# Summing a gate's modulation over partitions with one full-width TensorE product a stream, instead of quarter-width products and a trip through DRAM

## The chip, the cores and the metric

The kernel runs on one core of one Trainium2 chip. The metric is the device time of one execution in microseconds (us). The kernel before takes 1478.86 us, the median of 3 runs (1477.71 to 1479.12). TensorE is called PE here, VectorE DVE, ScalarE ACT, GpSimd POOL and SyncE SP, as in the profile. A wait of an instruction is given by the profile as idle time of its engine, with the instruction or transfer that ended it.

## The reference

The model is a two-layer trunk over 256 context tokens and 256 latent tokens of width 1024. Every layer has an attention part with three mixers (MLA, differential attention, sliding-window attention called SWA) and a SwiGLU part. Each part is modulated by six vectors that come from the condition:

```
def adaln(cond, w, b):
    return jnp.split(jax.nn.silu(cond) @ w + b, 6, axis=-1)

def modulate(h, shift, scale):
    return h * (1.0 + scale) + shift
# per layer: shift1, scale1, gate1, shift2, scale2, gate2
#   x = x + gate1 * rms_norm(mixers(...), attn_post_norm)
#   x = x + gate2 * rms_norm(swiglu(...), ffn_post_norm)
```

The change concerns the two gate vectors, number 2 and number 5 of the six. The kernel stores a gate already multiplied with its norm weight and with 32, the square root of 1024, so that the residual is one product more.

## The kernel before, in words

All matrix products of the blocks run on PE with the weights split into a high and a low part: three matmuls per product, recorded at lines L262, L263 and L264 and accumulated in PSUM (`psg`). Weight blocks are loaded by SP into `raw` buffers (L170), cast by ACT (L131, the high part) and subtracted by DVE (L132, the low part, both called `hl`). Only then can PE use them.

The modulation is computed on DVE beside this work, by the generator `ada_dve`. The weights of a vector's half (512 columns) come as four tiles `aw` of 128 partitions (L342 issues them on SP). Partition p and tile j hold rows of the weight matrix; DVE multiplies each with the activated condition of that partition and adds it into `acc` (L397 and L399), one 512-column accumulator for each stream (`ns` = 2: latent and context, or `ns` = 1 in the last layer's gates). What is left is the sum over the 128 partitions. `finish` does it: products with a 128 x 32 block of ones (L357) sum 256 columns each into 32 partitions of PSUM, and ACT copies the sums to SBUF (L359).

For shift and scale vectors the sums are then transposed on PE. For a gate the sum must stand on every partition. There `finish` writes one row per 256 columns to DRAM (L362), reads it back broadcast to 128 partitions into the tile `gw` (L371), and loads the bias and the norm weight in the same broadcast form into two buffers of the `work` pool (L375 and L376). All four transfers are issued by SP. Then DVE adds the bias (L379) and multiplies with 32 and the weight (L380).

The `work` pool has six buffers of 128 x 512 that all engines share in turn, for exponentials, normed products and the like. A buffer is handed on when its last reader has finished.

The order of the work is set by the order in which the program is written and by generators that yield costs in microseconds. `start_fill` starts one `ada_dve` run beside the main sequence, and `fillers` advances it by the cost of what PE has been given. There are four such runs. The first (layer 0, beside its mixers) makes vectors 4, 3 and gate 2 with two streams. The second (beside the SwiGLU of layer 0) makes gate 5 with two streams and vectors of layer 1. The third and fourth make gate 2 and gate 5 of layer 1 with one stream. So there are eight gate halves: four with two streams and four with one. A `finish` is itself a generator (`pend`): it is advanced by `next(pend, None)` between the `aw` tiles of the following half, at high priority, and after each step the run is charged 0.3, 0.3 and, for a gate, `1.0 * ns`.

Of the kernel before, what the change touches and what calls it, by code (L numbers as in the profile page):

```python
# [10 lines left out]
F32 = mybir.dt.float32  # L11
# [3 lines left out]
ALU = mybir.AluOpType  # L15
# [4 lines left out]
P = 128  # L20
D = 1024
# [66 lines left out]
def trunk(ctx: ExitStack, tc: tile.TileContext, x, cx, b_ada, attn_post,  # L88
          ffn_post, w_in, w_uq, w_ukv, diff_lambda, swa_sink,
          w_ba, w_bb, w_bc, w_o, w_gu, w_dn, const_a, const_b, ada_first, ada_rest, out, dram_in):  # L90
    nc = tc.nc
# [5 lines left out]
    dp = ctx.enter_context(tc.tile_pool(name="dp", bufs=1, space=DRAM))  # L97
# [4 lines left out]
    def bank(tag="g"):  # L102
        return pp.tile([P, 512], F32, tag=tag, bufs=BANKS[tag], name=f"ps{tag}")
# [7 lines left out]
    def work():  # L111
        return sp.tile([P, 512], F32, tag="w2", bufs=6, name="work")
# [4 lines left out]
    ident, sel_f = ca[:, 0:128], ca[:, 128:130]  # L117
# [4 lines left out]
    ones = cp.tile([P, P], F32, name="ones")  # L122
# [193 lines left out]
    mods = {}  # L316

    def mod_finish(l, kind, f0, m, pv):

        nf, ns = pv.shape[1:]  # L320
        o = l * 48 + kind * 8 + f0
        b = bt[:, o:o + nf].rearrange("p (f o) -> p f o", o=1).to_broadcast([P, nf, ns])
        mq = m[:, f0:f0 + nf, :ns]
        nc.vector.tensor_tensor(mq, pv, b, ALU.add)
        if kind in (1, 4):
            off = (VAP if kind == 1 else VFP) + 8 * l + f0
            w = vt[:, off:off + nf].rearrange("p (f o) -> p f o", o=1).to_broadcast([P, nf, ns])
            nc.vector.scalar_tensor_tensor(mq, mq, 1.0, w, ALU.add, ALU.mult)

    def mod_tile(kind):  # L330
        return cp.tile([P, KD, 2], F32, tag=f"mod{kind}", name=f"mod{kind}")

    def ada_dve(*jobs):


        H = D // 2
        todo = [(l, kind, ns, hf) for l, kind, ns in jobs for hf in range(2)]

        def raw(i, j):
            l, kind, _, hf = todo[i]  # L340
            w = sp.tile([P, 2, H], F32, tag="xt", bufs=2, name="aw")
            nc.sync.dma_start(w.rearrange("p k n -> p (k n)"), ada_rest[l, kind, hf, j])  # L342
            return w

        def finish(l, kind, ns, hf, acc):
            m = mods[l, kind]
            gate = kind in (2, 5)
            n = 64 * ns
            ps = bank("T")
            for g in range(2):  # L350
                for s in range(ns):
                    j = 32 * (2 * s + g if gate else ns * g + s)
                    if gate:
                        src = acc[:, s, g * 256:(g + 1) * 256]
                    else:
                        src = acc[:, s].rearrange("p (b g c) -> p b g c", b=2, g=2)[:, :, g]
                    nc.tensor.matmul(ps[j:j + 32, :256], lhsT=ones[:, :32], rhs=src, start=True, stop=True)  # L357
            sums = work()[:, :256]
            nc.scalar.copy(sums[:n], ps[:n, :256])  # L359
            if gate:  # L360
                row = dp.tile([2 * ns, 256], F32, name=f"row{l}_{kind}_{hf}")
                nc.sync.dma_start(row, sums[0:n:32])  # L362
            yield
            if not gate:
                ps = bank("T")
                for b in range(2):
                    nc.tensor.transpose(ps[:, b * n:(b + 1) * n], sums[:n, b * P:(b + 1) * P], ident[:n, :n])
                mod_finish(l, kind, 4 * hf, m, ps[:, :2 * n].rearrange("p (f s z) -> p f s z", s=ns, z=32)[:, :, :, 0])
                return
            mq = m[:, :ns, hf * H:(hf + 1) * H]  # L370
            nc.sync.dma_start(mq, row.rearrange("(s g) p -> s (g p)", s=ns).rearrange("(o s) n -> o s n", o=1).to_broadcast([P, ns, H]))  # L371
            bw = [work(), work()]
            w = attn_post if kind == 2 else ffn_post
            c0 = kind * D + hf * H
            nc.sync.dma_start(bw[0], b_ada[l:l + 1, c0:c0 + H].to_broadcast([P, H]))  # L375
            nc.sync.dma_start(bw[1], w[l:l + 1, hf * H:(hf + 1) * H].to_broadcast([P, H]))  # L376
            yield
            for s in range(ns):
                nc.vector.tensor_tensor(mq[:, s], mq[:, s], bw[0], ALU.add)  # L379
                nc.vector.scalar_tensor_tensor(mq[:, s], mq[:, s], 32.0, bw[1], ALU.mult, ALU.mult)  # L380

        nxt = raw(0, 0)
        pend = None
        for i, (l, kind, ns, hf) in enumerate(todo):
            if hf == 0:
                gate = kind in (2, 5)
                mods[l, kind] = bp.tile([P, 2, D], F32, tag="gw", bufs=1, name="gw") if gate else mod_tile(kind)
            acc = sp.tile([P, 2, H], F32, tag="acc", bufs=2, name="acc")
            for j in range(4):
                w = nxt  # L390
                if j < 3 or i + 1 < len(todo):
                    nxt = raw(i + j // 3, (j + 1) % 4)
                for k in range(2):
                    for s in range(ns):
                        sc = siluc[:, s, 2 * j + k:2 * j + k + 1]
                        if j == 0 and k == 0:
                            nc.vector.tensor_scalar(acc[:, s], w[:, k], sc, None, ALU.mult)  # L397
                        else:
                            nc.vector.scalar_tensor_tensor(acc[:, s], w[:, k], sc, acc[:, s], ALU.mult, ALU.add)  # L399
                    yield 0.76 * ns  # L400
                if j and pend is not None:
                    with tc.high_priority():
                        next(pend, None)
                    yield (0.3, 0.3, 1.0 * ns if kind in (2, 5) else 0.0)[j - 1]
            pend = finish(l, kind, ns, hf, acc)
        for _ in range(3):
            yield 2.0
            with tc.high_priority():
                next(pend, None)
# [3 lines left out]
    for t in range(4):  # L413
        src = cx if t < 2 else x
# [1023 lines left out]
    for l in range(DEPTH):  # L1438
# [20 lines left out]
        if l == 0:  # L1459
            later = [(30.0, lambda: start_fill(ada_dve((0, 4, 2), (0, 3, 2), (0, 2, 2)), FR[0]))]  # L1460
        else:
            later = ()
            start_fill(ada_dve((1, 2, 1)), FR[2])
# [12 lines left out]
        for i, t in enumerate(qts):  # L1476
            ch = L[l]["ch", qts[i - 1]] if i else None
            a, b = PRM["WO"][2 * l:2 * l + 2]
            drive(1, at=[(a, lambda: next(ch, None)), (b, lambda: next(ch, None))] if i else ())
        ch = L[l]["ch", qts[-1]]  # L1480
        if not last:
            drive(1, at=[(a, lambda: next(ch, None)) for a in PRM["WO"][4:]])
            start_fill(ada_dve((0, 5, 2), (1, 1, 2), (1, 0, 2), (1, 4, 1), (1, 3, 1)), FR[1])
        else:
            warm(WN[0])
            next(ch, None)
            next(ch, None)
            warm(WN[1])
            start_fill(ada_dve((1, 5, 1)), FR[3])
# [47 lines left out]
```

## Time and profile before

| what | value |
|---|---|
| median of 3 runs | 1478.86 us |
| the profiled execution, its own time | 1479.64 us |
| its span, first to last instruction | 1477.9 us |
| granted PE clock, mean over the span | 0.995 of full speed |
| PE busy | 1437.3 us, 97% |
| DVE busy | 969.3 us, 66% |
| ACT busy | 684.3 us, 46% |
| POOL busy | 175.8 us, 12% |

The shares are averages over stages that differ. A time in the rows below counts from the start of the span. Matmuls overlap in their pipeline, so what a matmul costs is read from the distance between the starts of the matmuls around it, not from its own duration. A float32 matmul call leaves two records, a split product one record in each of three lines.

### The profile page before, as it was taken

How to read it: one execution, taken by the hardware profiler on the slowest of the kernel's cores; microseconds unless marked ns; L12 is line 12 of the kernel's file. 1: busy time of each engine (PE TensorE's matmuls, PEld its weight loads, DVE VectorE, ACT ScalarE, POOL GpSimd, SP SyncE). 2: the span in 40 equal slices, each digit the busy share in tenths (PEclk: the TensorE clock that was granted, in tenths of full speed). 3: DMA queues.
4: the chain of work that ended last, by engine and by line, in shares of the span. 5: the costliest groups of instructions: out<-in, count | busy, mean ns of one | idle time of the engine just before them, and what ended most of it. 6: DMA issues, size and time to landing. Idle time of an engine off the chain costs nothing. (4 is left out here: it accounts for less than half of the span.)

```text
span 1477.9 us, 21889 instructions
## 1 busy us (share of the span) xinstructions
PE 1437.3 (97%) x8434; PEld 1213.7 (82%) x8434; DVE 969.3 (66%) x1646; ACT 684.3 (46%) x1265; POOL 175.8 (12%) x245
## 2 busy tenths in 40 slices
PE   8989999999999999999999999999999899999998
PEld 7867878777777889887778888878798899899986
DVE  4676777878785655879773224779577776666644
ACT  5576554444552355223222123765455655544443
POOL 1262001220000010000000000364013100100000
PEclk9999999999999999999999999999999999999999
DMA  9321322233223542666572324333242426566664
GB/s 351 123 80 43 115 86 100 103 112 128 86 86 129 185 143 98 215 216 213 198 230 99 100 95 151 126 109 130 100 137 90 161 101 221 170 226 217 215 202 161
DMA packets 62728, 216.16 MB, mean 146 GB/s; under 512 B 7048, under 2 KB 7584, under 8 KB 62624
## 3 DMA queue, kind: packets, MB, share of 16 engines
q1 hardware_dynamic: 61184, 210.05, 42.0%
q10 hardware_dynamic: 1440, 4.72, 0.8%
q8 instruction: 66, 1.08, 0.3%
q14 instruction: 38, 0.31, 0.1%
HBM read 209.48 MB, written 5.27 MB: 145 GB/s over the span
## 5 line engine op out<-in xcount | busy, mean ns | idle before, releaser
L262 PE MATMUL psg<-hT,hl 128*128 128x512 f32 (+1 forms) x1328 | 470.6, 354 | 0.0
L264 PE MATMUL psg<-hT,hl 128*128 128x512 f32 (+1 forms) x1328 | 449.2, 338 | 1.0 <-DVE hl L132 1.0
L263 PE MATMUL psg<-hT,hl 128*128 128x512 f32 (+1 forms) x1328 | 448.8, 338 | 0.3 <-DVE hT L460 0.3
L132 DVE TENSOR_TENSOR hl<-raw,hl 128x1024 fp32r<-128x1024 f32 (+2 forms) x251 | 311.0, 1239 | 209.4 <-ACT hl L131 208.7
L131 ACT CAST hl<-raw 128x1024 fp32r<-128x1024 f32 (+2 forms) x251 | 259.3, 1033 | 328.0 <-PE psg L264 172.5
L262 PEld LDWEIGHTS psg<-hT,hl 128*128 128x128 f32 x1328 | 252.4, 190 | 38.6 <-issue 15.4
L264 PEld LDWEIGHTS psg<-hT,hl 128*128 128x128 f32 x1328 | 252.2, 190 | 29.3 <-DVE hl L132 1.4
L263 PEld LDWEIGHTS psg<-hT,hl 128*128 128x128 f32 x1328 | 252.9, 190 | 25.8 <-issue 3.6
L399 DVE SCALAR_TENSOR_TENSOR acc<-aw,siluc,acc 128x512 f32<-128x512 f32 x224 | 165.0, 762 | 22.4 <-DMA aw<-in_ada_rest 21.1
L477 POOL TENSOR_SCALAR smy<-ssy 128x1 f32<-128x1 f32 x12 | 4.1, 339 | 709.7 <-ACT work L293 709.7
L673 ACT ACTIVATE work<-psS,nm 128x512 f32<-128x512 f32 (+1 forms) x96 | 59.1, 616 | 62.2 <-DVE nm L669 34.7
L669 DVE TENSOR_REDUCE nm<-psS 128x1 f32<-128x512 f32 (+1 forms) x96 | 56.9, 596 | 24.5 <-PE psS L735 18.1
L684 PE MATMUL psT<-ca,work 128*128 128x128 f32 x400 | 63.7, 274 | 6.2 <-DVE work L759 3.8
L262 PE MATMUL psg<-oT,hl 128*128 128x512 f32 (+1 forms) x192 | 68.2, 355 | 0.0
L264 PE MATMUL psg<-oT,hl 128*128 128x512 f32 (+1 forms) x192 | 64.9, 338 | 1.6 <-DVE hl L132 1.6
L263 PE MATMUL psg<-oT,hl 128*128 128x512 f32 (+1 forms) x192 | 64.7, 337 | 0.0
L684 PEld LDWEIGHTS psT<-ca,work 128*128 128x128 f32 x400 | 48.6, 141 | 16.9 <-issue 7.0
L262 PE MATMUL psg<-hl,hT 128*128 128x256 f32 (+1 forms) x168 | 57.1, 340 | 1.4 <-ACT hT L131 1.4
L673 ACT ACTIVATE work<-psS,nmd 128x512 f32<-128x512 f32 (+1 forms) x48 | 29.6, 617 | 44.2 <-DVE nmd L669 23.4
L264 PE MATMUL psg<-hl,hT 128*128 128x256 f32 (+1 forms) x168 | 48.0, 285 | 0.4 <-DVE hT L132 0.4
L263 PE MATMUL psg<-hl,hT 128*128 128x256 f32 (+1 forms) x168 | 47.7, 284 | 0.0
L735 PE MATMUL psS<-kT,qT 96*128 96x512 f32 (+1 forms) x96 | 44.0, 541 | 2.7 <-ACT work L673 2.5
(357 smaller groups left out, 2501.8 us busy)
## 6 DMA issues: line engine op xcount, KB each, us to landing
raw<-in_blocks SPq DMA_DIRECT2D x262, 512.0 KB, 3.5
aw<-in_ada_rest SPq DMA_DIRECT2D x80, 512.0 KB, 4.6
aw<-in_ada_first SPq DMA_DIRECT2D x16, 512.0 KB, 7.2
xd<-xt ACTq DMA_DIRECT2D x6, 512.0 KB, 2.7
xt<-xd SPq DMA_DIRECT2D x6, 512.0 KB, 4.5
raw<-in_blocks SPq DMA_DIRECT2D x8, 272.0 KB, 5.8
xt<-in_ctx SPq DMA_DIRECT2D x4, 512.0 KB, 3.8
gw<-row SPq DMA_DIRECT2D x4, 512.0 KB, 4.4
```

What stands on the lines that cost most here:

```text
L131: nc.scalar.copy(hi, src)
L132: nc.vector.tensor_tensor(lo, src, hi.bitcast(F32), ALU.subtract)
L262: nc.tensor.matmul(ps, lhsT=asl(a[0], k), rhs=bsl(b[0], k), start=st, stop=False)
L263: nc.tensor.matmul(ps, lhsT=asl(a[0], k), rhs=bsl(b[1], k), start=False, stop=False)
L264: nc.tensor.matmul(ps, lhsT=asl(a[1], k), rhs=bsl(b[0], k), start=False, stop=en)
L399: nc.vector.scalar_tensor_tensor(acc[:, s], w[:, k], sc, acc[:, s], ALU.mult, ALU.add)
L477: nc.gpsimd.tensor_scalar(sm, ss[:, 0:1], ss[:, 1:2], D * EPS, ALU.add, ALU.add)
L669: nc.vector.tensor_reduce(nm, ps[:, :nk], AX.X, ALU.max, negate=True)
L673: nc.scalar.activation(st["p"][:, :nk], ps[:, :nk], AF.Exp, bias=nm, accum_out=sm)
L684: nc.tensor.transpose(pt[:, k * P:(k + 1) * P], st["p"][:, k * P:(k + 1) * P], ident)
L735: nc.tensor.matmul(st["ps"][:, :nk], lhsT=q, rhs=k, start=z == 0, stop=z == len(ops) - 1 and mk is None)
```

## The change

A gate gets a `finish` of its own, `finish_gate`. It first issues the bias and weight rows, now on ACT's queue, into two `work` buffers. Then, for each stream, it yields once, multiplies the whole accumulator by a 128 x 128 block of ones in one float32 matmul of 512 columns, so that every partition of PSUM holds the sum, and lets DVE add the bias straight from PSUM and multiply as before. The ACT copy, the row in DRAM and its read-back are gone. The charge of the last step becomes 1.0 for one and for two streams. `finish` keeps the shift and scale vectors; what it does for them is the same.

```
+        def finish_gate(l, kind, ns, hf, acc):
+            mq = mods[l, kind][:, :ns, hf * H:(hf + 1) * H]
+            bw = [work(), work()]
...
+            nc.scalar.dma_start(bw[0], b_ada[l:l + 1, c0:c0 + H].to_broadcast([P, H]))
+            nc.scalar.dma_start(bw[1], w[l:l + 1, hf * H:(hf + 1) * H].to_broadcast([P, H]))
+            for s in range(ns):
+                yield
+                ps = bank("T")
+                nc.tensor.matmul(ps, lhsT=ones, rhs=acc[:, s], start=True, stop=True)
+                nc.vector.tensor_tensor(mq[:, s], ps, bw[0], ALU.add)
+                nc.vector.scalar_tensor_tensor(mq[:, s], mq[:, s], 32.0, bw[1], ALU.mult, ALU.mult)
...
-                    j = 32 * (2 * s + g if gate else ns * g + s)
-                    if gate:
-                        src = acc[:, s, g * 256:(g + 1) * 256]
...
-            if gate:
-                row = dp.tile([2 * ns, 256], F32, name=f"row{l}_{kind}_{hf}")
-                nc.sync.dma_start(row, sums[0:n:32])
             yield
...
-            mq = m[:, :ns, hf * H:(hf + 1) * H]
-            nc.sync.dma_start(mq, row.rearrange("(s g) p -> s (g p)", s=ns).rearrange("(o s) n -> o s n", o=1).to_broadcast([P, ns, H]))
-            bw = [work(), work()]
...
-            nc.sync.dma_start(bw[0], b_ada[l:l + 1, c0:c0 + H].to_broadcast([P, H]))
-            nc.sync.dma_start(bw[1], w[l:l + 1, hf * H:(hf + 1) * H].to_broadcast([P, H]))
-            yield
-            for s in range(ns):
-                nc.vector.tensor_tensor(mq[:, s], mq[:, s], bw[0], ALU.add)
-                nc.vector.scalar_tensor_tensor(mq[:, s], mq[:, s], 32.0, bw[1], ALU.mult, ALU.mult)
...
-                    yield (0.3, 0.3, 1.0 * ns if kind in (2, 5) else 0.0)[j - 1]
-            pend = finish(l, kind, ns, hf, acc)
+                    yield (0.3, 0.3, 1.0 if kind in (2, 5) else 0.0)[j - 1]
+            pend = (finish_gate if kind in (2, 5) else finish)(l, kind, ns, hf, acc)
```

In the changed kernel the new lines are L351 and L352 (the two loads on ACT), L356 (the product), L357 and L358 (the two DVE operations). Every line of the kernel before from L383 on has a number lower by 5 there: L673 becomes L668, L759 becomes L754, L399 becomes L394. On PE the matmuls outside the gate keep their order; only the gate's products stand later. Two places show what moves on the other engines.

The first place is ACT at the end of SWA in layer 0, where the first half of gate 2 is finished. L673 is the exponential of a score tile into a `work` buffer, L689 the copy of a transposed score tile, L750 (after: L745) the exponential of the sink. Before:

```order
L750 ACTIVATE es<-es 128x2
L1167 ACTIVATE work<-psg 128x512
L673 ACTIVATE work,sm_4481<-psS,nm_4482 128x512
L131 CAST hl<-raw 128x1024
L757 ACTIVATE work<-work,rsd 128x512
L359 COPY work<-psT 128x256
L689 COPY pp<-psT 128x4x128
```

After, at the same place:

```order
L668 ACTIVATE work,sm_4481<-psS,nm_4482 128x512
L351 DMA work<-in_b_ada 128x512
L352 DMA work<-in_attn_post_norm 128x512
L1162 ACTIVATE work<-psg 128x512
L745 ACTIVATE es<-es 128x2
L131 CAST hl<-raw 128x1024
L668 ACTIVATE work,sm_4481<-psS,nm_4482 128x512
L684 COPY pp<-psT 128x4x128
L752 ACTIVATE work<-work,rsd 128x512
```

The two loads take their `work` buffers before the last exponential of SWA takes its own, and that exponential now stands behind the cast of a weight block.

The same place on DVE: L759 (after: L754) scales the last exponential, which PE then transposes; L1220 (after: L1215) reads a product from PSUM. Before:

```order
L671 TENSOR_SCALAR nm_4482<-nm_4482,nsink 128x1
L749 TENSOR_TENSOR es<-nm_4482,sink 128x2
L691 COPY pp<-psT 128x4x128
L751 TENSOR_TENSOR sm_4481<-sm_4481,es 128x2
L753 RECIPROCAL rsd<-sm_4481 128x2
L759 TENSOR_SCALAR work<-work,rsd 128x512
L132 TENSOR_TENSOR hl<-raw,hl 128x1024
L1220 SCALAR_TENSOR_TENSOR work<-work,psg 128x512
```

After:

```order
L394 SCALAR_TENSOR_TENSOR acc<-aw,siluc,acc 128x512
L666 TENSOR_SCALAR nm_4482<-nm_4482,nsink 128x1
L394 SCALAR_TENSOR_TENSOR acc<-aw,siluc,acc 128x512
L744 TENSOR_TENSOR es<-nm_4482,sink 128x2
L686 COPY pp<-psT 128x4x128
L394 SCALAR_TENSOR_TENSOR acc<-aw,siluc,acc 128x512 x2
L132 TENSOR_TENSOR hl<-raw,hl 128x1024
L1215 SCALAR_TENSOR_TENSOR work<-work,psg 128x512
L746 TENSOR_TENSOR sm_4481<-sm_4481,es 128x2
L748 RECIPROCAL rsd<-sm_4481 128x2
L754 TENSOR_SCALAR work<-work,rsd 128x512
```

Four accumulations of the next half, the split of a weight block and the product of L1215 now stand ahead of the scaling of the last exponential.

The second place is DVE at the start of the differential mixer in layer 1. L818, L819, L821 and L822 (after: L813, L814, L816, L817) turn two exponentials into one difference, which PE transposes; L669 (after: L664) is a row maximum. Before:

```order
L669 TENSOR_REDUCE nmd<-psS 128x1 x3
L818 RECIPROCAL rsd<-sm_9670 128x2
L819 TENSOR_TENSOR rsd<-rsd,lam 128x1
L821 TENSOR_SCALAR work<-work,rsd 128x512
L822 SCALAR_TENSOR_TENSOR work<-work,rsd 128x512
L669 TENSOR_REDUCE nmd<-psS 128x1
L132 TENSOR_TENSOR hl<-raw,hl 128x1024
```

After:

```order
L664 TENSOR_REDUCE nmd<-psS 128x1 x3
L813 RECIPROCAL rsd<-sm_9643 128x2
L394 SCALAR_TENSOR_TENSOR acc<-aw,siluc,acc 128x512
L814 TENSOR_TENSOR rsd<-rsd,lam 128x1
L394 SCALAR_TENSOR_TENSOR acc<-aw,siluc,acc 128x512
L664 TENSOR_REDUCE nmd<-psS 128x1
L816 TENSOR_SCALAR work<-work,rsd 128x512
L664 TENSOR_REDUCE nmd<-psS 128x1
L813 RECIPROCAL rsd<-sm_9689 128x2
L817 SCALAR_TENSOR_TENSOR work<-work,rsd 128x512
```

Two accumulations and two row maxima moved in between the reciprocal and the difference.

## Rows read from the trace of the kernel before

**Rows 1.** The page's first part: engine, busy time (share), number of instructions.
```profile
PE 1437.3 (97%) x8434; PEld 1213.7 (82%) x8434; DVE 969.3 (66%) x1646; ACT 684.3 (46%) x1265; POOL 175.8 (12%) x245
```
**Rows 2.** Busy time by stretch: stretch and length, PE, PEld, DVE, ACT, POOL, clock, DMA.
```profile
610.00:790.00 180.00, 180.00 (x827) 141.83 (x827) 136.48 (x195) 53.05 (x73) 0.00 (x0) 1.00 0.62 208
1075.00:1160.00 85.00, 80.16 (x599) 75.14 (x599) 62.38 (x109) 44.83 (x80) 19.24 (x25) 1.00 0.42 132
```
**Rows 3.** PE in order of time: start, duration, operation; two-stream gate, one-stream finish, score product.
```profile
643.73 0.39 PE L264 MATMUL psg<-hT,hl 128*128 128x512 f32 x1
644.04 0.64 PE L357 MATMUL psT<-acc,ones 128*32 128x256 f32 x8
644.95 0.39 PE L263 MATMUL psg<-hT,hl 128*128 128x512 f32 x1
...
739.26 0.39 PE L264 MATMUL psg<-hT,hl 128*128 128x512 f32 x1
740.47 0.39 PE L263 MATMUL psg<-hT,hl 128*128 128x512 f32 x1
...
105.41 0.39 PE L263 MATMUL psg<-hT,hl 128*128 128x512 f32 x1
105.64 0.40 PE L264 MATMUL psg<-hT,hl 128*128 128x512 f32 x1
105.87 1.02 PE L735 MATMUL psS<-kT,qT 96*128 96x512 f32 x2
106.97 0.40 PE L263 MATMUL psg<-hT,hl 128*128 128x512 f32 x1
```
**Rows 4.** Three lines' instructions: ACT copy, DVE addition with its waits, ACT-issued load.
```profile
L359 ACT COPY work<-psT x20: 359/368/377, 236.6 to 1411.4; 128x256 f32<-128x256 f32 x12, 64x256 f32<-64x256 f32 x8
...
L379 DVE TENSOR_TENSOR gw<-gw,work 128x512 f32<-128x512 f32 x12 | 7.9, 689 | 12.7 <-DMA work<-in_b_ada 12.7
...
L1263 ACTq DMA_DIRECT2D xd<-xt x6: 326/326/343, 533.5 to 1277.0; - x6
```
**Rows 5.** End of SWA in layer 0: ACT, DVE and PE in order of time.
```profile
439.93 0.68 ACT L673 ACTIVATE work<-psS,nm 128x512 f32<-128x512 f32 x1
...
441.13 0.49 DVE L759 TENSOR_SCALAR work<-work,rsd 128x512 f32<-128x512 f32 x1
445.11 0.69 DVE L1220 SCALAR_TENSOR_TENSOR work<-work,psg 128x512 f32<-128x512 f32 x1 [2.22 <-PE psg L264]
...
443.64 0.65 PE L684 MATMUL psT<-ca,work 128*128 128x128 f32 x4
444.84 0.60 PE L684 MATMUL psT<-ca,work 128*128 128x128 f32 x4
```
**Rows 6.** First difference of layer 1: DVE and PE in order of time.
```profile
1074.04 0.75 DVE L822 SCALAR_TENSOR_TENSOR work<-work,rsd 128x512 f32<-128x512 f32 x1
1077.11 0.73 DVE L399 SCALAR_TENSOR_TENSOR acc<-aw,siluc,acc 128x512 f32<-128x512 f32 x1
...
1076.29 0.60 PE L684 MATMUL psT<-ca,work 128*128 128x128 f32 x4
```
**Rows 7.** DVE, ACT and PE where layer 1's gate 2, first half, is finished.
```profile
1092.58 0.69 DVE L379 TENSOR_TENSOR gw<-gw,work 128x512 f32<-128x512 f32 x1 [1.97 <-DMA work<-in_b_ada]
...
1093.31 0.69 ACT L673 ACTIVATE work<-psS,nmd 128x512 f32<-128x512 f32 x1 [1.95 <-DVE gw L379]
...
1094.23 0.47 PE L809 MATMUL psS<-dQA 128*128 128x512 f32 x1 [1.78 <-ACT work L673]
```
**Rows 8.** DVE and PE around its second half.
```profile
1129.50 0.01 DVE L640 LOAD_MASK_SELECT rsh<-psg  x1 [0.98 <-PE psg L264]
...
1148.43 0.39 PE L264 MATMUL psg<-oT,hl 128*128 128x256 f32 x1 [1.59 <-DVE hl L132]
```
**Rows 9.** ACT and PE after the last gate half.
```profile
1422.99 1.05 ACT L131 CAST hl<-raw 128x1024 fp32r<-128x1024 f32 x1 [5.18 <-DMA raw<-in_blocks]
...
1425.36 0.50 PE L263 MATMUL psg<-hl,aT 128*128 128x512 f32 x1 [0.30 <-DVE hl L132]
```

More of the change, by code (lines that the diff above doesn't have):

```diff
@@ L343, in raw @@
             return w
+        def finish_gate(l, kind, ns, hf, acc):
+            mq = mods[l, kind][:, :ns, hf * H:(hf + 1) * H]
+            bw = [work(), work()]
+            w = attn_post if kind == 2 else ffn_post
+            c0 = kind * D + hf * H
+            nc.scalar.dma_start(bw[0], b_ada[l:l + 1, c0:c0 + H].to_broadcast([P, H]))
[6 more added lines that the diff above has]
+                nc.vector.scalar_tensor_tensor(mq[:, s], mq[:, s], 32.0, bw[1], ALU.mult, ALU.mult)
         def finish(l, kind, ns, hf, acc):
             m = mods[l, kind]
-            gate = kind in (2, 5)
             n = 64 * ns
@@ L351, in finish @@
                 for s in range(ns):
-                    j = 32 * (2 * s + g if gate else ns * g + s)
-                    if gate:
-                        src = acc[:, s, g * 256:(g + 1) * 256]
-                    else:
-                        src = acc[:, s].rearrange("p (b g c) -> p b g c", b=2, g=2)[:, :, g]
+                    j = 32 * (ns * g + s)
+                    src = acc[:, s].rearrange("p (b g c) -> p b g c", b=2, g=2)[:, :, g]
                     nc.tensor.matmul(ps[j:j + 32, :256], lhsT=ones[:, :32], rhs=src, start=True, stop=True)
@@ L359, in finish @@
             nc.scalar.copy(sums[:n], ps[:n, :256])
-            if gate:
-                row = dp.tile([2 * ns, 256], F32, name=f"row{l}_{kind}_{hf}")
-                nc.sync.dma_start(row, sums[0:n:32])
             yield
[L364 to L369, printed above, removed]
-            mq = m[:, :ns, hf * H:(hf + 1) * H]
-            nc.sync.dma_start(mq, row.rearrange("(s g) p -> s (g p)", s=ns).rearrange("(o s) n -> o s n", o=1).to_broadcast([P, ns, H]))
-            bw = [work(), work()]
-            w = attn_post if kind == 2 else ffn_post
-            c0 = kind * D + hf * H
-            nc.sync.dma_start(bw[0], b_ada[l:l + 1, c0:c0 + H].to_broadcast([P, H]))
-            nc.sync.dma_start(bw[1], w[l:l + 1, hf * H:(hf + 1) * H].to_broadcast([P, H]))
-            yield
-            for s in range(ns):
-                nc.vector.tensor_tensor(mq[:, s], mq[:, s], bw[0], ALU.add)
-                nc.vector.scalar_tensor_tensor(mq[:, s], mq[:, s], 32.0, bw[1], ALU.mult, ALU.mult)
+            ps = bank("T")
+            for b in range(2):
+                nc.tensor.transpose(ps[:, b * n:(b + 1) * n], sums[:n, b * P:(b + 1) * P], ident[:n, :n])
+            mod_finish(l, kind, 4 * hf, m, ps[:, :2 * n].rearrange("p (f s z) -> p f s z", s=ns, z=32)[:, :, :, 0])
         nxt = raw(0, 0)
```

## The prediction

> **What bounds the kernel now.** I first read the page's busy shares: PE works 97% of the span, DVE 66%, ACT 46%, POOL 12% [rows 1]. So the sum is a sum over PE: what its queue gets more or less to do, and which of its few waits come or go. Next I read PE's busy time by stretch, to see in which stretches PE waits at all. The SwiGLU of layer 0, in which gate 5 of layer 0 is finished, shows PE busy for 180.00 of 180.00 us; the mixers of layer 1, with gate 2, 80.16 of 85.00 us [rows 2]. In the first, whatever is added to PE is added to the time; in the second 4.84 us of waiting can take something in or be taken away. Third came PE's timeline around the gate products, for their price, and last the waits of DVE, ACT and PE around each of the eight gate halves, to see who waits for whom.
>
> **PE's own work.** The starts of two split matmuls of 512 columns lie 0.23 us apart (105.41 to 105.64) [rows 3]. With the four quarter-width products of a two-stream gate between them, L264 to the second matmul behind it takes 644.95 - 643.73 = 1.22 us; less two ordinary distances, 0.46, the four cost 0.76 us. The two products of a one-stream finish cost 740.47 - 739.26 - 0.46 = 0.75 us [rows 3]. The row shown is a one-stream shift or scale vector; its products have the same shape and number as a one-stream gate's.
>
> The new product is 128 x 128 by 512 columns in float32. The trace of before has none. The nearest is the score product L735, 96 x 128 by 512 columns in float32: 106.97 - 105.64 - 0.46 = 0.87 us [rows 3]. I take 0.87, since columns and number type are the same and only the rows of the array differ. From below, the two records of a float32 call could cost no more than two split matmuls, 0.46; from above, the whole 1.33 us between those starts.
>
> A two-stream half goes from 0.76 to 2 x 0.87 = 1.74: +0.98. A one-stream half goes from 0.75 to 0.87: +0.12. Four halves of each kind: 3.9 + 0.5 = **+4.4 us**. At 0.46 a product this would be 12 x 0.46 - 4 x 0.76 - 4 x 0.75 = -0.5 us, at 1.33 it would be +9.9 us.
>
> What is surprising is that four quarter-width products cost what two cost [rows 3]: they ran beside each other, so the old form had its 1024 columns for the price of about 450. Counted by columns alone, four times 256 against two times 512, the change would cost PE nothing in a two-stream half, and the sum below would be lower by 3.9 us. The Trainium skill, "TensorEngine Tiling (Array Packing)", section Key Properties, says that column tiles of the array can execute in parallel and that a change of the tiling mode drains the array; the first half speaks against this change, and the trace agrees with it (0.76 for four, 0.75 for two).
>
> **Off PE.** Removed: eight ACT copies of at most 0.37 us, eight row writes and eight read-backs on SP [rows 4]. Sixteen bias and weight loads move from SP to ACT, where a load's issue takes 0.326 us [rows 4]: 16 x 0.326 - 8 x 0.37 = +2.3 us of ACT, an engine busy 46% of the span [rows 1]. I cost it at nothing; PE's stretches hide it, and if each pair stood in front of a cast or an exponential that PE waits for, it would be 8 x 0.65 = 5.2 us. DVE keeps its 12 additions and 12 products. That the addition now reads PSUM is not shown by this line; L1220 reads PSUM with the same 512 columns in 0.69 us [rows 5], as long as L379 from SBUF, 0.689 [rows 4]: no change. DVE's 12.7 us of waiting for the bias row in L379 [rows 4] ends, since the loads are issued before PE's product and not behind the read-back. Most of it hides behind PE now and saves nothing. Three places are different:
>
> 1. Gate 2 of layer 1, first half. DVE waits 1.97 us for the bias row at L379. The exponential L673 on ACT needs the `work` buffer that L379 frees and waits 1.95 us; PE needs that exponential's score bank and waits 1.78 us [rows 7]. With the bias row early this chain is gone. Around a stalled start PE loses some more than the gap; I take 1.9 us: **-1.9**. The bounds are 0 and -1.95.
>
> 2. Its second half. The old products stood at 1123.7, ahead of a product for which DVE's L640 waits 0.98 us, in a chain of rotary work (POOL, ACT, DVE) that ends in PE's wait of 1.59 us at 1148.43 [rows 8]. The new product stands at about 1138, in front of that wait, which takes in its 0.87. So the removed 0.75 passes on to the chain, and the +0.12 charged above for this half is not paid: **-0.9**. If DVE's two gate operations, now inside that chain, hold it up by 0.69 each, it is +0.5; if both the wait and the chain shorten, -1.6.
>
> 3. Behind the last gate half. ACT waits 5.18 us for a weight block whose load stood behind the row, the read-back and the two gate loads on SP, and PE waits 0.30 [rows 9]. With those four gone the load leaves earlier: **-0.5** with the slow restart; the bounds are 0 and -0.5.
>
> The change also adds two waits.
>
> 4. End of SWA in layer 0, gate 2, first half. The two gate loads hold two of six `work` buffers from about 438, so the last exponential has to wait for the buffer that PE's transposes at 443.64 release; before, it started at 439.93 [rows 5]. The transposes come 0.76 earlier without the old products, about 442.9, and end 0.65 later, 443.5. From the exponential to the end of L759 it took 441.13 + 0.49 - 439.93 = 1.69; with L1220, which now stands ahead on DVE, another 0.69: 445.9. PE wants to transpose this tile at 444.84 - 0.76 = 444.1 [rows 5]. It waits 1.8 us, and behind it in PE's queue stand all the split products: **+1.8**. The bounds are 0 (if the buffers turn over in another way) and 3.
>
> 5. Start of the differential mixer in layer 1. L822 ended at 1074.79; two accumulations of 0.73 and a row maximum of 0.69 come ahead of it: 1076.94. PE transposes its output at 1076.29, now 0.75 earlier because the gate's products before it have moved behind: 1075.54 [rows 6]. **+1.4**; the bounds are 0 (DVE has gained on PE by then) and 1.6.
>
> **Sum.** +4.4 - 1.9 - 0.9 - 0.5 + 1.8 + 1.4 = +4.3 us. The profiled execution took 1479.64 us (span 1477.9, with 1.7 around it), 0.8 above the median 1478.86. On the profiled execution that is 1483.9, on the median 1483.2; I predict the median. 0.2% is 3.0 us, about what a measurement of this kernel can tell from no change.
>
> **Rivals.**
> - *The two new waits don't come.* The products are paid, the old waits go, and 4 and 5 are 0: +1.1 us, 1480.0. For it: both waits are worked out from an order and not seen, and DVE loses 12.7 us of waiting, so it may be ahead of where I put it. Against it: in 4 a buffer really is short, whatever DVE does.
> - *Faster: layer 1's mixers close up.* If DVE, free of the gate's waits, lets the whole stretch run through, PE gets back the 4.84 us that it waits there [rows 2], in place of terms 1 and 2, the charge of its two gate halves with them (0.24); 4 and 5 stay away: 4.4 - 4.84 - 0.24 - 0.5 = -1.2, 1477.7. It decides if the POOL-bound rotary chain was held up by the gate and not by itself; the wait of 1.59 is for a weight split behind that chain [rows 8], which the change touches only by two DVE operations. With a product near 0.46 on top, -6.
> - *Slower still: ACT's queue.* The loads wait for a `work` buffer in ACT's queue, and behind them stand a cast and an exponential. If every pair holds up PE by its 0.65, the sum is 4.3 + 5.2 = +9.5, 1488.4. For it: at the first gate half the pair stands before the last exponential. Against: ACT is idle more than half of the time, and in the SwiGLU it is busy 53 of 180 us [rows 2].
> - *The change doesn't do what it says* would need products that stay quarter-width; the new order shows 12 products of 512 columns, so I give it no chance.
>
> **How the numbers follow.** The forecast has 0.42, its own range 1481.5 to 1485.5 (term 4 or 5 off by its bound). The rival without new waits has 0.30, the closed-up mixers 0.14, ACT's queue 0.14. Slower by over 3.0 us: nearly all of the forecast, 0.37, and all of the last rival, 0.14: 0.51. Faster by over 3.0 us: the closed-up case with a cheaper product or more waits gone, 0.10. The rest, 0.39, is within. For 8 in 10 the range goes from 1477.5, which takes in the second rival's own value, to 1487.5.
>
> **What would show it.** A float32 product of 128 x 128 by 512 should stretch the distance of its neighbours by 0.87 us, and PE's busy time should grow by some 4.4 us. In the SwiGLU stretch no PE wait should appear and the time should grow by 2 us there. PE's transposes at about 444 and 1075.5 should each show a wait of 1.4 to 1.8 us for DVE. PE's wait of 1.78 us and the one of 0.30 should be gone. The forecast is wrong if the product costs 0.5 or less, or if the two transposes start without a wait.

## Result and the profile after

The changed kernel takes 1486.76 us, the median of 6 runs (1485.61 to 1489.96), against 1478.80 us of the kernel before on the same chip (6 runs, 1476.28 to 1481.33): a ratio of 1.0055, 95% interval 1.0044 to 1.0067, so 8.0 us slower. Forecast were 4.3 us. The profiled execution took 1486.67 us, 7.0 more than the profiled one of before. Medians and intervals, here and below, are of the runs in the fast state; one run of early_loads_old_product (1579.71 us) and one of f32r_product (3036.95 us) are left out.

The page's first part, engine by engine as in [rows 1]:

```profile
PE 1442.2 (97%) x8410; PEld 1218.0 (82%) x8410; DVE 970.9 (65%) x1646; ACT 681.5 (46%) x1257; POOL 175.2 (12%) x245
```

PE is busy 4.9 us longer; the rest of the 7.0 us must be waits, and they can't be seen in shares. The price of the new product, in PE's timeline, around a two-stream gate half in the SwiGLU of layer 0 (start, duration, operation; beside [rows 3]):

```profile
629.10 0.39 PE L264 MATMUL psg<-hT,hl 128*128 128x512 f32 x1
629.33 1.02 PE L356 MATMUL psT<-acc,ones 128*128 128x512 f32 x2
629.78 0.80 PE L262 MATMUL psg<-hT,hl 128*128 128x512 f32 x1
630.42 0.40 PE L263 MATMUL psg<-hT,hl 128*128 128x512 f32 x1
```

630.42 - 629.10 - 0.46 = 0.86 us: the product costs what the score product of before cost.

The end of SWA in layer 0, beside [rows 5]: ACT's last exponential and its neighbours, then DVE, PE and POOL.

```profile
439.43 1.03 ACT L131 CAST hl<-raw 128x1024 fp32r<-128x1024 f32 x1
442.42 0.69 ACT L668 ACTIVATE work<-psS,nm 128x512 f32<-128x512 f32 x1 [1.96 <-PE psT L679]
...
443.14 0.69 DVE L1215 SCALAR_TENSOR_TENSOR work<-work,psg 128x512 f32<-128x512 f32 x1 [0.79 <-PE psg L264]
443.74 0.15 DVE L746 TENSOR_TENSOR sm<-sm,es 128x2 f32<-128x2 f32 x1
...
444.13 1.32 DVE L754 TENSOR_SCALAR work<-work,rsd 128x512 f32<-128x512 f32 x1
...
441.73 0.60 PE L679 MATMUL psT<-ca,work 128*128 128x128 f32 x4
...
445.60 1.09 PE L679 MATMUL psT<-ca,work 128*128 128x128 f32 x4 [2.57 <-DVE work L754]
...
443.91 1.26 POOL L1217 TENSOR_TENSOR acc<-acc,work 128x512 f32<-128x512 f32 x1 [21.98 <-DVE sm L746]
```

The exponential waits 1.96 us for PE's transposes at 441.73, which release a `work` buffer, as forecast. PE then stands still for 2.57 us. Two things in these rows were not forecast: L754 takes 1.32 us where L759 took 0.49 [rows 5], and the transposes behind the stop take 1.09 instead of 0.60. The second is the clock. Busy time by stretch (length, PE, PEld, DVE, ACT, POOL, granted clock, DMA):

```profile
446.00:449.00 3.00, 3.00 (x10) 2.46 (x9) 0.69 (x1) 0.00 (x0) 0.00 (x0) 0.50 0.00 0
1173.00:1175.00 2.00, 2.00 (x9) 1.81 (x9) 1.08 (x5) 1.39 (x3) 0.00 (x0) 0.50 0.04 14
```

Behind the stop PE ran at 0.50, that is 1.2 GHz, and again for some 3 us behind a wait of 1.96 us that ended at 1171.88. Before had the same wait, ended at 1165.79, and kept its clock there. But before had a stretch at half the clock that the changed kernel did not have, behind a wait of 3.03 us:

```profile
291.50:294.50 3.00, 3.00 (x9) 2.54 (x10) 3.00 (x6) 1.53 (x3) 0.00 (x0) 0.50 0.00 0
```

Over the whole span both profiles have the same mean clock, 0.995.

The other places, on PE: the wait that the old charge did not have, the first difference of layer 1 [rows 6], the two halves of layer 1's gate 2 [rows 7, 8] (for the second also three rows of DVE) and the end [rows 9]. Each row stands by itself, and what lies between them is left out.

```profile
434.42 0.74 PE L730 MATMUL psS<-sk,sQ 128*128 128x512 f32 x2 [0.75 <-ACT work L668]
1083.85 0.63 PE L679 MATMUL psT<-ca,work 128*128 128x128 f32 x4 [0.90 <-DVE rsd L814]
1100.74 0.40 PE L804 MATMUL psS<-dQA 128*128 128x512 f32 x1
1143.43 1.02 PE L356 MATMUL psT<-acc,ones 128*128 128x512 f32 x2
1146.78 0.44 PE L697 MATMUL psT<-ca,work 128*128 128x128 f32 x2 [2.33 <-DVE oT L135]
1146.24 0.48 DVE L135 SCALAR_TENSOR_TENSOR oT<-psT,dnw,oT 128x256 fp32r<-128x256 f32 x1
1148.92 0.68 DVE L357 TENSOR_TENSOR gw<-psT,work 128x512 f32<-128x512 f32 x1
1150.53 0.69 DVE L358 SCALAR_TENSOR_TENSOR gw<-gw,work 128x512 f32<-128x512 f32 x1
1158.33 0.39 PE L264 MATMUL psg<-hT,hl 128*128 128x256 f32 x1 [0.44 <-DVE hl L132]
1432.35 0.39 PE L263 MATMUL psg<-hl,aT 128*128 128x512 f32 x1
```

The waits of 1.78 [rows 7], of 1.59 [rows 8] and of 0.30 us [rows 9] are gone; 0.90 and 2.33 are new. At 0.90 the profile names L814; L817, whose result PE transposes there, ends at 1083.70.

The matmuls outside the gate stand in the same order in both kernels, but for eight pairs of small transposes of shift and scale sums between 670 and 780, so each one's start in the one timeline less its start in the other is the delay up to there. How it grows:

| start before | start after | delay | what lies between (change of the delay) |
|---|---|---|---|
| 425.81 | 423.49 | -2.3 | the stretch up to here, without a gate: clock and order, see below |
| 436.32 | 435.06 | -1.3 | new wait of 0.75 (+1.1) |
| 444.05 | 442.08 | -2.0 | old products gone from here (-0.7) |
| 445.19 | 446.34 | +1.2 | stop of 2.57 (+2.7), the transposes behind it at half the clock (+0.4) |
| 446.67 | 449.03 | +2.4 | half the clock (+1.2) |
| 481.41 | 486.59 | +5.2 | four new products, one half's old ones gone (+2.8) |
| 654.50 | 661.70 | +7.2 | gate 5: four new products, two halves' old ones gone (+2.0) |
| 1069.86 | 1076.46 | +6.6 | old products of layer 1's gate 2 gone (-0.6) |
| 1076.64 | 1084.23 | +7.6 | new wait of 0.90 (+1.0) |
| 1084.45 | 1092.90 | +8.5 | new product (+0.9) |
| 1094.77 | 1101.21 | +6.4 | wait of 1.78 gone (-2.0) |
| 1124.75 | 1130.07 | +5.3 | old products and a wait of 0.20 gone (-1.1) |
| 1138.23 | 1146.98 | +8.8 | new product and new wait of 2.33 (+3.4) |
| 1152.24 | 1158.33 | +6.1 | waits of 0.33 and 1.59 gone, 0.67 now 0.44 (-2.7) |
| 1173.05 | 1180.27 | +7.2 | half the clock, less a wait of 0.23 that goes (+1.1) |
| 1425.36 | 1432.35 | +7.0 | last gate: +0.2; wait of 0.30 gone (-0.4) |

The first line holds nothing of the gate: 0.95 of it comes between 97.85 and 102.97, where both kernels' PE runs at 0.5 for a while after a wait and the profiled execution of the changed one got its clock back sooner, and 1.28 comes between 291 and 295, where before alone ran at 0.5. So in this pair the clock gave back 2.2 us before the gate's first product and took 2.7 us behind it: the net is 0.5 of the 7.0.

### The profile page after: what moved, and what is told of

It reads as the page before. It is cut to its first block, busy times and chain, and to the rows that moved or that the text cites. A ratio compares the mean times of both kernels' runs of the same rounds, so it can differ in the third digit from the quotient of the medians.

```text
span 1484.7 us, 21801 instructions
## 1 busy us (share of the span) xinstructions
PE 1442.2 (97%) x8410; PEld 1218.0 (82%) x8410; DVE 970.9 (65%) x1646; ACT 681.5 (46%) x1257; POOL 175.2 (12%) x245
## 5 line engine op out<-in xcount | busy, mean ns | idle before, releaser
L394 DVE SCALAR_TENSOR_TENSOR acc<-aw,siluc,acc 128x512 f32<-128x512 f32 x224 | 163.4, 755 | 21.0 <-DMA aw<-in_ada_rest 19.7
L668 ACT ACTIVATE work<-psS,nm 128x512 f32<-128x512 f32 (+1 forms) x96 | 59.1, 616 | 64.1 <-DVE nm L664 33.5
L664 DVE TENSOR_REDUCE nm<-psS 128x1 f32<-128x512 f32 (+1 forms) x96 | 57.0, 596 | 22.5 <-PE psS L730 16.3
L668 ACT ACTIVATE work<-psS,nmd 128x512 f32<-128x512 f32 (+1 forms) x48 | 29.6, 617 | 44.1 <-DVE nmd L664 29.3
```

Of the source, the lines that this page charges most:

```text
L664: nc.vector.tensor_reduce(nm, ps[:, :nk], AX.X, ALU.max, negate=True)
L668: nc.scalar.activation(st["p"][:, :nk], ps[:, :nk], AF.Exp, bias=nm, accum_out=sm)
```

## The experiments

Every kernel was timed beside the kernel before on the same chip, 29 runs with a median of 1479.77 us for no_work_buffers, old_charge, early_loads_old_product and f32r_product and of 1479.18 us for own_buffers_on_sp, charge_alone, f32r_old_charge and changed_again. Differences below are of medians against that; the ratios and their intervals are not quotients of the medians and differ from them by up to 0.15%.

**No buffer of the shared pool** (no_work_buffers), the changed kernel with:

```
-            bw = [work(), work()]
+            gb = sp.tile([P, H], F32, tag="gb", bufs=1, name="gb")
-            nc.scalar.dma_start(bw[0], b_ada...)
-            nc.scalar.dma_start(bw[1], w[...])
+            for s in range(ns):
+                nc.scalar.dma_start(mq[:, s], b_ada...)
+            nc.scalar.dma_start(gb, w[...])
```

> The changed kernel, but the gate finish takes no buffer of the shared work pool: the bias row goes straight into the gate tile (once for each stream) and the weight row into one buffer of its own. My theory: the change's 8.0 us are the float32 products (about 4.7) and a PE stop at the end of SWA in layer 0 (about 4.3: a wait of 2.57 us, a slow restart and half the PE clock for 3 us behind it), with the rest near -1; the stop comes because the two gate loads hold buffers that the last exponential needs. So here the stop is gone and the time is 1482.5 us (1481.5 to 1483.5). Rival 1: the stop comes from the four accumulations that DVE now does ahead of the scaling of that exponential; they still stand there, and the time stays at 1486 to 1487. Rival 2: the products cost all of it; also 1486 to 1487, though the stop is gone.

Measured: 1491.05 us (+11.3; ratio 1.009, 1.0069 to 1.0112). A miss, though the stop was gone (no PE wait over 0.25 us between 437 and 449). The start of ACT's timeline tells a part of why:

```profile
0.72 2.03 ACTq L352 DMA_DIRECT2D gw<-in_b_ada  x4
2.78 0.65 ACTq L353 DMA_DIRECT2D gb<-in_attn_post_norm  x1
3.46 1.28 ACT L125 ACT_TABLE_LOAD   x1 [3.46 <-issue]
...
7.36 0.63 ACT L293 ACTIVATE work<-xt 128x512 bf16<-128x512 f32 x1 [2.15 <-DMA xt<-in_ctx]
```

With nothing to hold them, the loads of layer 0's gates were put at the head of ACT's queue. The first square of the inputs ran at 7.36, in the changed kernel at 4.75, and PE's first split product that had waited there started at 22.82 instead of 19.47. The experiment had changed two things. The late start, 3.4 us, does not explain all of the 11.3: these six runs also had a mean granted clock of 0.9927, against 0.9953 of the kernel before, and spread from 1487.74 to 1496.37 us.

**The same with the loads on SP** (own_buffers_on_sp), whose order is the program's:

```
-                nc.scalar.dma_start(mq[:, s], b_ada...)
+                nc.sync.dma_start(mq[:, s], b_ada...)
```

> As no_work_buffers (no buffer of the shared pool held), but the gate loads are issued on SP, whose queue keeps the program's order. In no_work_buffers ACT's queue had the first gate's three loads moved to the very start of the kernel, since nothing held them there any more; the first cast of the inputs came 2.6 us later and PE's first split product 3.4 us later. My theory: that move hid the gain, and the held buffers alone make the stop at the end of SWA; with the loads on SP the start is the old one, the stop is gone and the time is 3 to 4 us above the kernel before: 1482.5 to 1484 us. Rival: the loads' own traffic costs, wherever they are issued; then 1486 or more.

Measured: 1483.10 us (+3.9; 1.0024, 1.0015 to 1.0034). ACT's last exponential now starts without a wait and PE waits 0.17 us:

```profile
438.89 0.68 ACT L669 ACTIVATE work<-psS,nm 128x512 f32<-128x512 f32 x1
...
443.41 0.63 PE L680 MATMUL psT<-ca,work 128*128 128x128 f32 x4 [0.17 <-DVE work L755]
```

So without the held buffers the stop does not come. The wait of 0.90 us in layer 1 is gone here, too. The four accumulations are still early in DVE's order here (one of them, waiting for its weights until 442.12, even stands in front of the scaling), and they cost 0.17.

**The old charge** (old_charge), the changed kernel with:

```
-                    yield (0.3, 0.3, 1.0 if kind in (2, 5) else 0.0)[j - 1]
+                    yield (0.3, 0.3, 1.0 * ns if kind in (2, 5) else 0.0)[j - 1]
```

> The changed kernel with the charge of the gate's last step back at 1.0 for each stream, so that the later steps of the first two fill runs fall where they did before. My theory: the stop at the end of SWA needs both the held buffers and the earlier accumulations; with the old charge the last exponential takes its buffer first, the stop is gone, and the products stay: 1482.5 us (1481.5 to 1483.5). Rival: the buffers alone decide, the stop stays, 1486 to 1487.

Measured: 1482.40 us (+2.6; 1.0023, 1.0011 to 1.0035). The last exponential runs without a wait at 435.95, beside the first load (435.89) and ahead of the second, and the transposes that had waited 2.57 start without a wait at 440.13. The wait at 434.42 is gone too. Two rows of ACT, exponential and second load:

```profile
435.95 0.68 ACT L668 ACTIVATE work<-psS,nm 128x512 f32<-128x512 f32 x1
...
439.63 0.34 ACTq L352 DMA_DIRECT2D work<-in_attn_post_norm  x1
```

So the stop needs both, the buffers and the earlier place that the lower charge gave the gate's step.

**The charge alone** (charge_alone), the kernel before with `1.0` in place of `1.0 * ns`.

> The kernel before with only the charge of the gate's last step lowered to 1.0 for two streams, as in the changed kernel. My theory: the charge moves later steps of the first two fill runs up by 2 us, and without held buffers no stop comes of it: within 1 us of the kernel before, 1479 to 1481 us. Rival: the charge alone makes the stop at the end of SWA (old_charge was 5 us faster than the changed kernel); then 1483 to 1484 us.

Measured: 1480.21 us (+1.0; 1.0011, 0.9999 to 1.0024, which takes in no change). No stop at 444, but one row of PE shows the wait that the changed kernel has at 434.42:

```profile
437.28 0.73 PE L735 MATMUL psS<-sk,sQ 128*128 128x512 f32 x2 [1.12 <-ACT work L673]
```

It is in all seven profiles with the low charge (0.75 to 1.87 us) and in none of the four with the old one.

**The early loads with the old product** (early_loads_old_product), the kernel before with:

```
+                bw = [work(), work()]
+                nc.scalar.dma_start(bw[0], b_ada...)
+                nc.scalar.dma_start(bw[1], w[...])
                 row = dp.tile(...)
...
-            nc.sync.dma_start(bw[0], ...)
-            nc.sync.dma_start(bw[1], ...)
```

> The kernel before, with its quarter-width products and its trip through DRAM, but the gate loads issued early and on ACT as in the changed kernel. My theory: the loads alone cost nothing, since the charge of the last step is still 1.0 for each stream and the order at the end of SWA is that of before; the wait of 1.78 us of PE in layer 1 stays, because DVE still waits there for the read-back. 1478.8 us (1477.5 to 1480). Rival: the early hold of two work buffers or ACT's queue is what costs; then 1481 to 1484.

Measured: 1480.90 us (+1.1; 1.0016, 1.0005 to 1.0028). A miss, between theory and rival. The wait of 1.78 us did go (so what DVE waited for had been the bias, not the read-back), and two others came: 2.40 us at 1078.89 for L822, behind an accumulation that waits for its weights, and 0.93 at 1424.93.

```profile
1076.73 0.75 DVE L399 SCALAR_TENSOR_TENSOR acc<-aw,siluc,acc 128x512 f32<-128x512 f32 x1 [2.69 <-DMA aw<-in_ada_rest]
...
1078.00 0.74 DVE L822 SCALAR_TENSOR_TENSOR work<-work,rsd 128x512 f32<-128x512 f32 x1
```

So this place of layer 1, forecast as a cost of the new order, is one that a shift of the accumulations hits without the new product, too.

**A cheaper product** (f32r_product), the changed kernel with:

```
+    ones_r = cp.tile([P, P], F32R, name="ones_r")
+    nc.gpsimd.tensor_copy(ones_r, ones)
...
-                nc.tensor.matmul(ps, lhsT=ones, rhs=acc[:, s], ...)
+                nc.tensor.matmul(ps, lhsT=ones_r, rhs=mq[:, s], ...)
...
+                            o = mods[l, kind][:, s, hf * H:(hf + 1) * H] if gate and j == 3 and k == 1 else acc[:, s]
-                            nc.vector.scalar_tensor_tensor(acc[:, s], w[:, k], sc, acc[:, s], ...)
+                            nc.vector.scalar_tensor_tensor(o, w[:, k], sc, acc[:, s], ...)
```

> The changed kernel, but the last accumulation of a gate writes a rounded float32r value (into the gate tile) and the product over partitions is one float32r matmul with float32r ones; less precise. My theory: a float32 product costs 0.87 to 0.90 us of PE, a float32r one 0.23, all on the path: 12 x 0.65 = 7.8 us less than the changed kernel, 1479.0 us (1478 to 1480), with the stop at the end of SWA still there. Rival: the products' columns fall in waits of PE anyway and only the waits around them cost; then 1485 to 1487.

Measured: 1481.00 us (+1.2; 1.0007, 0.9993 to 1.002). Against the changed kernel's +8.0 and +9.5 (below) that is 6.8 to 8.3 us less; the 7.8 of the expectation lies between, while the time itself is 1 us over its range. The stop is there with 2.57 us, and the clock kept its 1.0 behind it.

**Both edits** (f32r_old_charge).

> The changed kernel with both edits that helped: the rounded float32r product and the old charge. My theory: they add, since one acts on PE's columns and the other on the stop at the end of SWA: 1.2 us above before, less 4.3 to 5.4: 1475.5 to 1477 us, 3 to 4 us faster than the kernel before. Rival: with cheap products PE reaches the chains of layer 1 earlier and waits there instead; then 1478 to 1480 us.

Measured: 1474.85 us (-4.3; 0.9974, 0.9962 to 0.9986), faster than both kernels and a little below the expected range. PE's timeline shows the product in line with its neighbours:

```profile
625.38 0.39 PE L266 MATMUL psg<-hT,hl 128*128 128x512 f32 x1
625.61 0.39 PE L358 MATMUL psT<-gw,ones_r 128*128 128x512 f32 x1
625.83 0.39 PE L264 MATMUL psg<-hT,hl 128*128 128x512 f32 x1
```

It costs 0.22 us, 0.64 less than the float32 one. The step from old_charge (+2.6) to here is 6.9 us for twelve products, 12 x 0.64 = 7.7 if all were on the path: nearly all are.

**The changed kernel again** (changed_again).

> The changed kernel itself, on the chip of these experiments. My theory: the stop at the end of SWA is in the order and comes again with 2.5 to 2.6 us; the half PE clock behind a wait of 2 us or more comes in some executions and not in others (in the profile of the changed kernel behind 444 and 1170, in f32r_product not behind the same stop but at 1143). 7 to 9 us above the kernel before: 1486.5 to 1488.5 us. Rival: the half clock belongs to the stop; then it stands behind 444 again and not elsewhere.

Measured: 1488.70 us (+9.5; 1.0066, 1.0051 to 1.008), slightly over the expectation. The stop is there with 2.57 us. The clock behind it is not half this time; it is half behind the wait of 2.33 us in layer 1 (the transposes behind the stop, then two stretches, with the granted clock in the column before the DMA share):

```profile
445.87 0.63 PE L679 MATMUL psT<-ca,work 128*128 128x128 f32 x4 [2.57 <-DVE work L754]
...
446.00:449.00 3.00, 3.00 (x16) 2.54 (x16) 0.69 (x1) 0.00 (x0) 0.00 (x0) 1.00 0.00 0
1147.00:1151.00 4.00, 4.00 (x23) 4.00 (x23) 3.47 (x6) 1.69 (x4) 2.15 (x2) 0.57 0.31 105
```

So the half clock doesn't belong to this stop; it comes behind one of the waits of about 2 us or more, in one execution here and in the other there. Without it the stop puts PE back by 2.73 us, 0.16 more than its length.

The runs' mean granted clocks say how much of a median it is: 0.9940 in these six runs, 0.9954 in the 29 of the kernel before, 0.9953 in the twelve of own_buffers_on_sp. Among those 29 runs the time rises by 1.15 us for each 0.001 of clock that is missing (by 1.0 among the other 29), so by an estimate some 1.5 us of the 9.5 here are clock.

**One addition moved from POOL to DVE** (sum_on_dve), a single run:

```
-                        nc.gpsimd.tensor_tensor(a, a, g, ALU.add)
+                        (nc.vector if i == 6 else nc.gpsimd).tensor_tensor(a, a, g, ALU.add)
```

> The changed kernel with one POOL addition (L1217, the one at 443.91) done on DVE, where it falls ahead of the scaling L754. In the profile of the changed kernel L754 took 1.32 us instead of 0.49, and ended 0.28 us after this POOL addition of 1.26 us that had begun before it. My theory: the two engines got in each other's way; without the POOL addition L754 takes 0.49 again, comes about 0.6 later, and PE's stop at the end of SWA is 2.57 - 0.83 + 0.6 = 2.3 to 2.4 us. Rival: L754 is slow here for another reason; it takes 1.32 again and the stop is 3.1 to 3.2 us.

Measured: the profile shows L754 at 0.49 us and PE's stop at 2.27 us; the one run took 1487.65 us.

```profile
444.21 0.69 DVE L1217 TENSOR_TENSOR acc<-acc,work 128x512 f32<-128x512 f32 x1
...
445.01 0.49 DVE L754 TENSOR_SCALAR work<-work,rsd 128x512 f32<-128x512 f32 x1
...
445.64 0.63 PE L679 MATMUL psT<-ca,work 128*128 128x128 f32 x4 [2.27 <-DVE work L754]
```

It started 0.88 us later than in the changed kernel and still ended within 0.05 us of it. The 0.83 us of L754 were POOL's. They could have been read before: in the trace of before L759 takes 1.35 us where a POOL addition of 1.29 us has begun ahead of it, earlier in the same layer.

```profile
390.72 1.29 POOL L1222 TENSOR_TENSOR acc<-acc,work 128x512 f32<-128x512 f32 x1 [20.86 <-DVE sm L751]
390.95 1.35 DVE L759 TENSOR_SCALAR work<-work,rsd 128x512 f32<-128x512 f32 x1
```

## Why the prediction was right

The direction, the range (1477.5 to 1487.5) and the main terms held; the sum was 3.7 us short. That the time fell inside the range owes something to luck: it lies 0.7 us below its upper end and above the forecast's own 1481.5 to 1485.5, and changed_again's 1488.70 lies outside. Term by term, with the delay table:

- *PE's own work, +4.4*: the product cost 0.86 us for the 0.87 taken from L735, and the twelve together cost about 4.7 (lines 444, 481, 654, 1070, 1084 and the last gates, with 0.1 for the second half of layer 1's gate 2; these lines take in small shifts of other matmuls, and 12 x 0.87 less the 0.77 by which the delay falls at each of the eight old halves is 4.3). f32r_product and f32r_old_charge show that nearly all of it is on the path. The other reading, by columns alone (no cost in a two-stream half), is refuted: gate 5 of layer 0, in a stretch without a PE wait, cost 2.0 us, as forecast. The quarter-width tiles had indeed run beside each other.
- *ACT's loads and DVE's PSUM operand, 0*: ACT was busy 2.8 us less, not 2.3 more, since issues don't count as busy; its queue cost nothing that a trace shows. L357 reads PSUM in 0.688 us, L379 read SBUF in 0.689 [rows 4].
- *1, -1.9*: -2.0. The chain from bias row to PE's wait was read rightly, and early_loads_old_product shows that the bias row was the end of it.
- *2, -0.9*: the half came to -0.4 (1094.77 to 1152.24: -1.1 + 3.4 - 2.7), against -0.8 forecast for it with the +0.12. The removed 0.75 did pass on to the chain, and the new product's 0.87 was not paid. What failed is that DVE's gate operations hold up nothing. The second, L358 at 1150.53, stands between two operations of the chain (L135) and puts the rest of it back by 0.7; the forecast had named this as its other case. The wait of 2.33 was not forecast either. The product takes one of the two `psT` banks until L357 has read it at 1148.92, the other is held by L135 at 1146.24, and the transposes L697 wait for it; before, L702 at 1138.09 found a bank free. It costs little, since PE waits for the chain in any case: 0.33 + 1.59 + 0.67 before became 2.33 + 0.44.
- *3, -0.5*: -0.4.
- *4, +1.8*: +2.7, the term that was mis-sized most. Mechanism and place were right: the exponential waits for the buffer that the transposes release, and own_buffers_on_sp and old_charge show that the stop needs the held buffers and the early place of the loads. The working took 0.49 us for L759; beside POOL's addition it took 1.32. 2.57 - 0.83 = 1.74, the forecast's 1.8. Another 0.16 is the start behind the stop, which I had counted in term 1 but not here.
- *5, +1.4*: +1.0, with the mechanism of the forecast, two accumulations and two row maxima ahead of L817.
- *Left out*: the lower charge has no term of its own. charge_alone shows 1.0 us, not clear of noise, with a wait of ACT's buffer at 434 to 437. In the two profiles it is +1.1 less the wait of 0.5 us at 425 that went: +0.6.
- *Left out*: the clock. The half clock behind 445.60 and 1171.88 cost 1.6 and 1.1 us in the profile (before lost 2.2 more than the changed kernel ahead of that); in changed_again it stood elsewhere. I had costed a stop by its length alone.

The steady terms add up to 4.7 - 2.0 - 0.4 - 0.4 + 2.7 + 1.0 + 0.6 = +6.2 us; with the clock's net 0.5 that is near the 7.0 of the two profiles. The medians are +8.0 and +9.5. In changed_again some 1.5 us of the difference are clock, by the estimate above, and 1.8 us are left open; at the first +8.0 the 1.8 us above the sum can't be split, since the clocks of the kernel before are not on record there. Why own_buffers_on_sp is 5.6 us faster than changed_again can be put together from the record: some 1.5 of clock, 2.4 of the stop (2.57 against 0.17), 1.0 for the wait of 0.90 in layer 1, 0.7 for the wait at 434 (1.87 against 1.20).

Of the rivals, the one without the new waits had named rightly what term 5 depends on, but both waits came, with 2.57 and 0.90 us. The mixers of layer 1 did not close up: PE waits 3.75 us of 85 there (1082 to 1167), after 4.84. The one on ACT's queue (+9.5) was nearest in size, but not in its mechanism: nothing in the changed kernel's trace waits for a gate load to land. The change does what it says: the eight trips through DRAM are gone, and the time that they took had been hidden except for about 2.4 us.

## What to carry to other kernels

On an engine that is busy 97% of the time, a wait that is removed elsewhere is worth only what that engine waited for it; add up the columns that the change gives it first, at the price of the nearest product of the same number type in the same kernel. A buffer from a shared pool that is taken early for a load is a wait for whoever takes the next one: look at who is next in the queue order, and whether an own buffer is to be had. The same goes for a PSUM bank that a product takes. A load that nothing holds can be put to the head of its queue, so when an experiment frees one, look at the start of the timeline first.

## What the runs showed of the hardware

- DVE's tensor-scalar operation of 128 x 512 at the end of SWA (L759, after: L754) takes 0.49 us alone, and 1.35 (before, 390.95), 1.32 (after, 444.13) and 1.32 (changed_again, 444.41) when it begins inside a POOL addition of 1.26 to 1.29 us; in all three it ends 0.3 us after that addition, and with the addition on DVE it takes 0.49. The Trainium skill, "SBUF — State Buffer", section "Summary: rules for kernel authors", says that with DVE in its two-port mode the second of the two engines to issue blocks until the first has finished; the runs agree in that DVE, the second, lost 0.83 us, and none shows in which mode it was.
- PE's granted clock falls from 2.4 to 1.2 GHz behind some waits of 2 to 3 us, for some 3 us (once 6.8, in before behind 97); behind 445.60 and 1171.88 this cost 1.6 and 1.1 us. The same wait of 1.96 us (ended at 1165.79 and 1171.88) was followed by it in the changed kernel's profile and not in that of before, and the stop of 2.57 us in one profile of the changed kernel and not in the other.
- A bias row issued by ACT landed after 4.0 us (median of eight), by SP after 5.4 in the kernel before and 4.4 (median of twelve) in own_buffers_on_sp; the loads' places and neighbours differ too, so this is not the engine's doing alone.
